# A two-layer attention trunk: x in quarters and a written order at the head, a shorter chain of norm steps at the end

## Chip, cores and metric

One core of one Trainium2 chip runs the whole kernel. The metric is device time in microseconds (us) of one execution, the median over several. Engines: TensorE (PE), VectorE (DVE), ScalarE (ACT), GpSimd (POOL), and SyncE (SP), which here only issues transfers.

## What is computed

256 tokens of width 1024 pass through two layers and a final norm, all in float32:

```python
for layer in range(2):
    h = rmsnorm(x, g_mix)
    proj = h @ w_in                      # 1024 x 7244: q,k,v of three attentions, indexer, gates
    A = stick_breaking_attention(...)    # 8 heads
    B = forgetting_attention(...)        # 8 heads, softmax with cumulative forget bias
    C = indexed_sparse_attention(...)    # rotary, indexer picks the top 64 keys per token
    y = sum(sigmoid(gate_b) * (branch_b @ w_branch[b]) for b in A, B, C)
    x = x + y @ w_out
    x = x + relu(rmsnorm(x, g_mlp) @ w_up) ** 2 @ w_down
return rmsnorm(x, g_final)               # x * (mean(x*x) + 1e-6) ** -0.5 * g_final
```

## The kernel before, in words

**Tiling.** The 256 tokens are two blocks j of 128; x lives on the chip as two halves h of its columns (`xh`, 512 columns each, both token blocks). A matrix product splits each float32 operand into a rounded part and a remainder (`whi`, `wlo` for weights, `xTh`, `xTl` for transposed activations) and sums three products (`mm3`, L117): high by high, high by low, low by high. ACT makes the high part by a copy (L91 for weights, L173 for x), DVE the low part by a subtraction (L92, L174). Weights come in `raw` tiles of four 128-row blocks (`w_rows`, L99; four buffers) and are split two row blocks at a time into four `whi` and four `wlo` buffers.

**The head.** SP issues x's first half as two transfers (L64), the norm gain (L66), the first weight tile row block by row block (`loads=4`, L104), x's second half (L62), then the next weight tiles. `norm_in` (L157) transposes x on PE, four 128x128 blocks to a PSUM tile (L168), ACT and DVE make `xTh` and `xTl` with the gain folded in, and ACT sums squares (L178). `rstd_of` (L182) makes the reciprocal root on GpSimd in three steps. The first products are the 1100 columns of C's projections in three groups: 364 and 368 columns together (`stream_groups`, L242; four row blocks k of the first group, four of the second, then the other four of each), then 368 alone (L244). `ct_done` (L237) copies each finished group out of PSUM on ACT, scaled by the norm. Behind them stand the small constants of the rotary embedding (L246 to L307).

**What sets the order.** Each engine issues its instructions in one fixed sequence. That sequence is made by a planner when the program is built: it simulates the program and picks, for an engine that comes free, by the order of the source and by what is ready. A region marked `manual_schedule(engines=...)` makes the named engines issue that region's instructions as they are written; where instructions from outside the region fall among them stays the planner's. Before, only one such region exists per layer, for PE alone (L651).

**The tail.** In layer 1's last product (`w_down`, L711) the second column half finishes token block 0 first, then block 1 (`split_last`). For each block DVE adds the residual (L713), ACT sums squares (L716), DVE multiplies by the final gain (L717), GpSimd adds the two halves' sums, makes the mean and takes the power (L185, L186, L188), ACT scales one column half (L723) and DVE the other (L725), and SP issues both outputs (L724, L726).

## Time and profile before

| | |
|---|---|
| median of 3 runs | 888.93 us (888.49 to 889.79) |
| profiled execution | 889.98 us, span 888.3 us |
| PE busy | 873.0 us, 98% of the span |
| DVE, ACT, POOL busy | 621.6, 531.1, 113.9 us |
| DMA | 150.97 MB, mean 170 GB/s |

The span runs from the first to the last instruction of the profiled execution. A busy PE is not PE at its peak, since the ends of pipelined matmuls are modelled; the start of one matmul to the start of the next shows the rate.

### The profile page before, as it was taken

How to read it: one execution, taken by the hardware profiler on the slowest of the kernel's cores; microseconds unless marked ns; L12 is line 12 of the kernel's file. 1: busy time of each engine (PE TensorE's matmuls, PEld its weight loads, DVE VectorE, ACT ScalarE, POOL GpSimd, SP SyncE). 2: the span in 40 equal slices, each digit the busy share in tenths (PEclk: the TensorE clock that was granted, in tenths of full speed). 3: DMA queues.
4: the chain of work that ended last, by engine and by line, in shares of the span. 5: the costliest groups of instructions: out<-in, count | busy, mean ns of one | idle time of the engine just before them, and what ended most of it. 6: DMA issues, size and time to landing. Idle time of an engine off the chain costs nothing.

```text
span 888.3 us, 13911 instructions
## 1 busy us (share of the span) xinstructions
PE 873.0 (98%) x5342; PEld 789.1 (89%) x5342; DVE 621.6 (70%) x1008; ACT 531.1 (60%) x874; POOL 113.9 (13%) x216
## 2 busy tenths in 40 slices
PE   7999999999999999999999999999999999999996
PEld 7998998888889999888899989988888999998885
DVE  5899787978766666545468987789876676664552
ACT  6766886776455555444365758677755655553442
POOL 2300321234001000000011014022600100000001
PEclk9999999999999999999999999999999999999998
DMA  8744544354555555555466463453346555555521
GB/s 288 244 147 143 190 143 143 116 169 143 190 190 164 176 183 190 190 189 190 137 208 195 139 197 136 143 189 128 106 150 232 169 190 190 190 188 192 190 95 48
DMA packets 102482, 150.97 MB, mean 170 GB/s; under 512 B 2928, under 2 KB 58256, under 8 KB 102416
## 3 DMA queue, kind: packets, MB, share of 16 engines
q1 hardware_dynamic: 102416, 150.08, 51.5%
q8 instruction: 42, 0.69, 0.3%
q14 instruction: 24, 0.20, 0.1%
HBM read 149.02 MB, written 1.05 MB: 169 GB/s over the span
## 4 chain that ended last, share of the span: by engine, by line
PE 92%; DVE 4%; ACT 1%; DMA 1%; issue 1%; SPq 0%; POOL 0%; POOLq 0%; ACTq 0%
PE mm L120 26%; PE mm L119 26%; PE mm L121 26%; PE av L454 2%; PE pT L438 2%; PE at L120 1%; PE at L121 1%; PE at L119 1%; DVE wlo L92 1%; DVE qs L145 1%; PE xtp L168 1%; ACT qs L143 1%; DMA x<-in_x_dram 1%; PE za L347 0%; PE yTp L579 0%
## 5 line engine op out<-in xcount | busy, mean ns | idle before, releaser
L92 DVE TENSOR_TENSOR wlo<-raw,whi 128x1024 fp32r<-128x1024 f32 (+3 forms) x289 | 347.8, 1206 | 201.0 <-ACT whi L91 199.4
L91 ACT ACTIVATE whi<-raw 128x1024 fp32r<-128x1024 f32 (+3 forms) x289 | 298.5, 1036 | 253.1 <-PE mm L121 142.4
L121 PE MATMUL mm<-xTh,wlo 128*128 128x256 f32 x752 | 214.0, 285 | 0.0
L119 PE MATMUL mm<-xTh,whi 128*128 128x256 f32 x752 | 213.8, 284 | 0.0
L120 PE MATMUL mm<-xTl,whi 128*128 128x256 f32 x752 | 213.6, 284 | 0.0
L119 PEld LDWEIGHTS mm<-xTh,whi 128*128 128x128 f32 x752 | 144.2, 192 | 0.2
L120 PEld LDWEIGHTS mm<-xTl,whi 128*128 128x128 f32 x752 | 144.2, 192 | 0.2
L121 PEld LDWEIGHTS mm<-xTh,wlo 128*128 128x128 f32 x752 | 144.2, 192 | 0.0
L120 PE MATMUL mm<-wlo,xTh 128*128 128x512 f32 (+2 forms) x320 | 122.7, 384 | 0.5 <-DVE wlo L92 0.5
L121 PE MATMUL mm<-whi,xTl 128*128 128x512 f32 (+2 forms) x320 | 121.6, 383 | 0.0
L119 PE MATMUL mm<-whi,xTh 128*128 128x512 f32 (+2 forms) x320 | 119.4, 383 | 0.3 <-ACT xTh L173 0.3
L121 PE MATMUL mm<-whi,ul 128*128 128x512 f32 x256 | 99.7, 389 | 0.0
L120 PE MATMUL mm<-wlo,uh 128*128 128x512 f32 x256 | 99.6, 389 | 0.0
L119 PE MATMUL mm<-whi,uh 128*128 128x512 f32 x256 | 99.2, 389 | 0.0
L120 PEld LDWEIGHTS mm<-wlo,xTh 128*128 128x128 f32 x320 | 61.0, 191 | 10.3 <-DVE wlo L92 1.3
L119 PEld LDWEIGHTS mm<-whi,xTh 128*128 128x128 f32 x320 | 60.9, 190 | 10.2 <-ACT xTh L173 0.7
L121 PEld LDWEIGHTS mm<-whi,xTl 128*128 128x128 f32 x320 | 60.8, 190 | 9.0
L185 POOL TENSOR_TENSOR ms<-ss 128x2 f32<-128x2 f32 (+1 forms) x6 | 4.3, 718 | 474.4 <-ACT junk L178 297.7
L121 PEld LDWEIGHTS mm<-whi,ul 128*128 128x128 f32 x256 | 48.1, 188 | 10.0
L120 PEld LDWEIGHTS mm<-wlo,uh 128*128 128x128 f32 x256 | 48.1, 188 | 10.0
L119 PEld LDWEIGHTS mm<-whi,uh 128*128 128x128 f32 x256 | 48.1, 188 | 9.7
L487 POOL TENSOR_SCALAR e<-e,rs 128x128 f32<-128x128 f32 x64 | 43.2, 693 | 27.2 <-DVE rs L484 27.2
(215 smaller groups left out, 1274.0 us busy)
## 6 DMA issues: line engine op xcount, KB each, us to landing
raw<-in_w_in_dram SPq DMA_DIRECT2D x48, 1024.0 KB, 5.0
raw<-in_w_up_dram SPq DMA_DIRECT2D x32, 1024.0 KB, 5.1
raw<-in_w_down_dram SPq DMA_DIRECT2D x32, 1024.0 KB, 5.0
raw<-in_w_branch_dram SPq DMA_DIRECT2D x12, 1024.0 KB, 5.0
raw<-in_w_out_dram SPq DMA_DIRECT2D x8, 1024.0 KB, 5.0
raw<-in_w_in_dram SPq DMA_DIRECT2D x8, 736.0 KB, 5.4
raw<-in_w_in_dram SPq DMA_DIRECT2D x3, 728.0 KB, 4.3
out_dram<-x SPq DMA_DIRECT2D x4, 256.0 KB, 2.2
```

The lines of the kernel that those rows point to most:

```text
L91: act.activation(h3[:, i:i + m], raw[:, i:i + m], AF.Copy)
L92: dve.tensor_sub(l3[:, i:i + m], raw[:, i:i + m], h3[:, i:i + m].bitcast(F32))
L119: pe.matmul(o, ah, bh, start=start, stop=False)
L120: pe.matmul(o, ah, bl, start=False, stop=False)
L121: pe.matmul(o, al, bh, start=False, stop=stop)
L143: act.activation(dst[half(i), :, i, :], src[half(i)], AF.Copy, scale=scale)
L145: dve.scalar_tensor_tensor(dst[half(1 - i), :, i, :], src[half(i)], scale, dst[half(i), :, i, :].bitcast(F32), op0=OP.mult, op1=OP.subtract)
L168: pe.transpose(p[:, i * 256 + j * 128:i * 256 + j * 128 + 128], xs[j][h][:, c:c + 128], ident)
L185: pool.tensor_add(ms, ss[:, :, 0], ss[:, :, 1])
L438: pe.transpose(p[:, q * 128:q * 128 + 128], e[:, i, q * 128:q * 128 + 128], ident)
L454: pe.matmul(o[:, c + c0:c + 256], v, p[:, a:b], start=s == 0 and n == 0, stop=s == 1 and n == 1)
L487: pool.tensor_scalar(e[:, i, c:c + n], e[:, i, c:c + n], rs[:, i, j:j + 1], 1.0, op0=OP.mult, op1=OP.mult)
```

## The change

Head:
- x comes in four quarters of 256 columns, both token blocks in one transfer (`load_x(queue, q)`).
- The gain, x's second quarter and two of the eight first weight row blocks are issued by ACT, the rest by SP; the four row blocks of both first groups are separate transfers (`head_rows`), except the last two of the second group, which share one. Each row block is split alone, when the stream comes to it (`ws[i]()`).
- A `manual_schedule` region for PE, ACT and DVE reaches from the first transposes through both column groups and the rotary constants. In it, `head_mid` says where the remaining transposes, the squares, the norm and its row form stand between the matmuls. The third group of 368 columns is now written behind the region.
- All transposes of the head use the `pt` PSUM buffers, where one half used `at`.

Tail:
- Block sums of the second column half are made in two quarters of 256 columns; the squares go to four columns of sums `fs`, one of which already has `D * EPS` added; one DVE operation adds three numbers, GpSimd takes one power (the factor 32 = sqrt(1024) is folded into the gain once).
- The scalings of both blocks are written behind both blocks' sums; ACT issues the half that it scaled, SP the one that DVE scaled.

```diff
@@ -56,14 +56,15 @@
 
     xh = [const.tile([128, 2, 512], F32, name=f"x{h}") for h in range(2)]
     xs = [[xh[h][:, j, :] for h in range(2)] for j in range(2)]
-    gload = const.tile([16, 128], F32, name="gload", tag="gload")
-
-    def load_x(h):
-        dma.dma_start(xh[h], AP(x, h * 512, [[D, 128], [128 * D, 2], [1, 512]]))
-
-    for j in range(2):
-        dma.dma_start(xh[0][:, j, :], AP(x, j * 128 * D, [[D, 128], [1, 512]]))
-    dma.dma_start(gload, AP(g_mix, 0, [[128, 16], [1, 128]]))
+    gload = const.tile([48, 128], F32, name="gload", tag="gload")
+
+    def load_x(queue, q):
+
+        queue.dma_start(xh[q // 2][:, :, (q % 2) * 256:(q % 2) * 256 + 256],
+                        AP(x, q * 256, [[D, 128], [128 * D, 2], [1, 256]]))
+
+    act.dma_start(gload[0:16], AP(g_mix, 0, [[128, 16], [1, 128]]))
+    load_x(dma, 0)
 
 
     ident = const.tile([128, 128], F32, name="ident")
@@ -71,42 +72,55 @@
     pool.affine_select(ident, ident, [[-1, 128]], OP.not_equal, 1.0, base=0, channel_multiplier=1)
     gT = const.tile([128, 32], F32, name="gT")
 
-    def g_cols(src, c):
+    def g_cols(r, c):
         p = at_tile("gps")
-        pe.transpose(p[:, 0:16], src, ident[0:16, 0:16])
+        pe.transpose(p[:, 0:16], gload[r:r + 16], ident[r:r + 16, r:r + 16])
         dve.tensor_copy(gT[:, c:c + 16], p[:, 0:16])
 
-    g_cols(gload, 0)
     mhalf = const.tile([128, 2], F32, name="mhalf")
     pool.memset(mhalf, -0.5)
 
 
...
+
+    def head_rows(off, n):
+
+        raw = raw_tile(4, n)
+        two = {}
+
+        def load(queue, i, m=1):
+            queue.dma_start(raw[:, i:i + m, :], AP(w_in, off + i * 128 * COLS, [[COLS, 128], [128 * COLS, m], [1, n]]))
+
+        def part(i):
+            if i % 2 == 0:
+                two[i // 2] = [wp.tile([128, 1024], F32R, name=t, tag=t, bufs=4) for t in ("whi", "wlo")]
+            h, l = [t[:, i % 2 * n:i % 2 * n + n] for t in two[i // 2]]
+            act.activation(h, raw[:, i], AF.Copy)
+            dve.tensor_sub(l, raw[:, i], h.bitcast(F32))
+            return h, l
+
+        return load, [lambda i=i: part(i) for i in range(4)]
 
     def w_cols(src, off, rs):
 
@@ -159,8 +173,8 @@
         xt = pair_tiles(8, "xT", 8)
         ss = small.tile([128, 2, 2], F32, name="ss")
 
-        def part(h):
-            for kp in range(2):
+        def part(h, kps=(0, 1), squares=True):
+            for kp in kps:
                 p = banks[h]("xtp")
                 for i in range(2):
                     for j in range(2):
@@ -173,7 +187,7 @@
                     act.activation(hi, p[:, i * 256:i * 256 + 256], AF.Copy, scale=g)
                     dve.scalar_tensor_tensor(lo, p[:, i * 256:i * 256 + 256], g, hi.bitcast(F32),
                                              op0=OP.mult, op1=OP.subtract)
-            for j in range(2):
+            for j in range(2 * squares):
                 junk = small.tile([128, 512], mybir.dt.bfloat16, name="junk", tag="junk", bufs=1)
                 act.activation(junk, xs[j][h], AF.Square, accum_out=ss[:, j, h:h + 1])
 
@@ -197,7 +211,7 @@
         o = [[t(), t()] for t in (mm_tile, at_tile)[:len(groups)]]
         for k0 in range(0, nk, 4):
             for g, (off, n) in enumerate(groups):
-                ws = first if first and not (k0 or g) else w_rows(src, off, rs, k0, n)
+                ws = list(first[g]) if first and not k0 else w_rows(src, off, rs, k0, n)
                 order = [(i, j) for i in range(4) for j in range(2)]
                 end = k0 + 4 == nk
                 if split_last and end:
@@ -206,6 +220,8 @@
                     if mid is not None:
                         mid(k0, g, q)
                     k = k0 + i
+                    if callable(ws[i]):
+                        ws[i] = ws[i]()
                     mm3(o[g][j][:, :n], blk(lhs, k, j * 128, j * 128 + 128), ws[i], k == 0, k == nk - 1)
                 if done is not None and end:
                     done(g, o[g])
@@ -214,38 +230,73 @@
     att = None
     for layer in range(DEPTH):
         wi0 = layer * D * COLS
+        cgs = [(736, 364), (0, 368)]
+        rstd = rb = rhalf = None
         if layer == 0:
-            wfirst = w_rows(w_in, C0 + 736, COLS, 0, 364, loads=4)
-            load_x(1)
-            xt, ss, part = norm_in(0, (at_tile, pt_tile))
-            part(0)
-            part(1)
-        rstd = rstd_of(ss)
+            head = [head_rows(C0 + c, n) for c, n in cgs]
+            (load0, _), (load1, _) = head
+            load0(act, 0)
+            load0(dma, 1)
+            load_x(act, 1)
+            load0(dma, 2)
+            load0(act, 3)
+            load1(dma, 0)
+            load1(dma, 1)
+            load1(dma, 2, 2)
+            load_x(dma, 2)
+            load_x(dma, 3)
+            xt, ss, part = norm_in(0, (pt_tile, pt_tile))
+            order = tc.manual_schedule(engines={mybir.EngineType.PE, mybir.EngineType.Activation, mybir.EngineType.DVE})
+            order.__enter__()
+            g_cols(0, 0)
+            part(0, (0,), False)
+
         with tc.tile_pool(name=f"att{layer}", bufs=1, reuse_waits="tile") as att:
             work = att
 
-            rp = at_tile("rp")
-            for j in range(2):
-                pe.transpose(rp[:, j * 128:j * 128 + 128], rstd[:, j:j + 1].to_broadcast([128, 128]), ident)
-            rb = small.tile([128, 272], F32, name="rb", tag="rb", bufs=1)[:, 0:256]
-            act.activation(rb, rp[:, 0:256], AF.Copy)
-
-            rhalf = small.tile([128, 2], F32, name="rhalf", tag="rhalf", bufs=1)
-            pool.tensor_scalar(rhalf, rstd, 0.5, 1.0, op0=OP.mult, op1=OP.mult)
+            def norms():
+
+                nonlocal rstd, rhalf
+                rstd = rstd_of(ss)
+                rhalf = small.tile([128, 2], F32, name="rhalf", tag="rhalf", bufs=1)
+                pool.tensor_scalar(rhalf, rstd, 0.5, 1.0, op0=OP.mult, op1=OP.mult)
+
+            def norm_row():
+
+                nonlocal rb
+                rp = pt_tile("rp")
+                for j in range(2):
+                    pe.transpose(rp[:, j * 128:j * 128 + 128], rstd[:, j:j + 1].to_broadcast([128, 128]), ident)
+                rb = small.tile([128, 272], F32, name="rb", tag="rb", bufs=1)[:, 0:256]
+                act.activation(rb, rp[:, 0:256], AF.Copy)
+
+            def head_mid(k0, g, q):
+                if (k0, g, q) == (0, 0, 2):
+                    part(0, (1,), False)
+                if (k0, g, q) == (0, 1, 4):
+                    part(1, (0, 1), False)
+                if (k0, g, q) == (0, 1, 2):
+                    part(0, ())
+                if (k0, g, q) == (0, 1, 7):
+                    part(1, ())
+                    norms()
+                if (k0, g, q) == (4, 1, 4):
+                    norm_row()
+
+            if layer:
+                norms()
+                norm_row()
 
             ct = att.tile([128, 2, 1152], F32, name="ct", tag="G", bufs=1)[:, :, 0:CN]
             def ct_done(c0, n, o):
                 for j in range(2):
                     act.activation(ct[:, j, c0:c0 + n], o[j][:, :n], AF.Copy, scale=rstd[:, j:j + 1])
 
-            cgs = [(736, 364), (0, 368)]
             stream_groups(xt, 8, w_in, [(wi0 + C0 + c, n) for c, n in cgs], COLS,
-                          done=lambda g, o: ct_done(*cgs[g], o), first=wfirst if layer == 0 else None)
-            ct_done(368, 368, stream_tok(xt, 8, w_in, wi0 + C0 + 368, COLS, 368))
-
+                          done=lambda g, o: ct_done(*cgs[g], o), first=None if layer else [h for _, h in head],
+                          mid=None if layer else head_mid)
             if layer == 0:
-                gload2 = const.tile([16, 128], F32, name="gload2", tag="gload")
-                dma.dma_start(gload2, AP(g_mlp, 0, [[128, 16], [1, 128]]))
+                dma.dma_start(gload[32:48], AP(g_mlp, 0, [[128, 16], [1, 128]]))
                 pos = const.tile([128, 2], I32, name="pos")
                 dma.dma_start(pos, AP(positions, 0, [[1, 128], [128, 2]]))
                 bfg = const.tile([128, DEPTH, NH], F32, name="bfg")
@@ -304,7 +355,10 @@
                 dve.tensor_scalar(rot[:, :, 0, :], trig[:, :, 0, :], -1.0, None, op0=OP.mult)
                 dve.tensor_copy(rot[:, :, 1, :], trig[:, :, 0, :])
 
-                g_cols(gload2, 16)
+                g_cols(32, 16)
+                order.__exit__(None, None, None)
+
+            ct_done(368, 368, stream_tok(xt, 8, w_in, wi0 + C0 + 368, COLS, 368))
 
 
             for c, nh in ((QI, 5), (QC, 10)):
@@ -704,26 +758,39 @@
             if last:
                 gfb = mlp.tile([128, D], F32, name="gfb")
                 dma.dma_start(gfb, AP(g_final, 0, [[0, 128], [1, D]]))
-                ss = small.tile([128, 2, 2], F32, name="ss")
+
+                act.activation(gfb, gfb, AF.Copy, scale=32.0)
+                fs = mlp.tile([128, 2, 4], F32, name="fs")
+                ms = mlp.tile([128, 2], F32, name="fms")
+                rl = mlp.tile([128, 2], F32, name="frstd")
             else:
                 xt, ss, part = norm_in(layer * 8 + 8, (at_tile, pt_tile))
             for cg in range(2):
                 o = stream_tok(uT, 32, w_down, layer * DFF * D + cg * 512, D, 512, split_last=last and cg == 1)
-                for j in range(2):
-                    dve.scalar_tensor_tensor(xs[j][cg], o[j], r2[:, j:j + 1], xs[j][cg], op0=OP.mult, op1=OP.add)
-                    if last:
+                if not last:
+                    for j in range(2):
+                        dve.scalar_tensor_tensor(xs[j][cg], o[j], r2[:, j:j + 1], xs[j][cg], op0=OP.mult, op1=OP.add)
+                    part(cg)
+                    continue
+                for j in range(2):
+                    steps = 2 if cg else 1
+                    n = 512 // steps
+                    for h in range(steps):
+                        xv = xs[j][cg][:, h * n:h * n + n]
+                        dve.scalar_tensor_tensor(xv, o[j][:, h * n:h * n + n], r2[:, j:j + 1], xv, op0=OP.mult, op1=OP.add)
                         junk = small.tile([128, 512], mybir.dt.bfloat16, name="junk", tag="junk", bufs=1)
-                        act.activation(junk, xs[j][cg], AF.Square, accum_out=ss[:, j, cg:cg + 1])
-                        dve.tensor_mul(xs[j][cg], xs[j][cg], gfb[:, cg * 512:cg * 512 + 512])
-                if not last:
-                    part(cg)
-                for j in range(2):
-                    if last and cg == 1:
-                        rl = rstd_of(ss[:, j:j + 1, :])
-                        act.activation(xs[j][1], xs[j][1], AF.Copy, scale=rl)
-                        dma.dma_start(AP(out, j * 128 * D + 512, [[D, 128], [1, 512]]), xs[j][1])
-                        dve.tensor_scalar(xs[j][0], xs[j][0], rl, None, op0=OP.mult)
-                        dma.dma_start(AP(out, j * 128 * D, [[D, 128], [1, 512]]), xs[j][0])
+                        act.activation(junk[:, :n], xv, AF.Square, accum_out=fs[:, j, cg + h:cg + h + 1])
+                    dve.tensor_mul(xs[j][cg], xs[j][cg], gfb[:, cg * 512:cg * 512 + 512])
+                    if cg == 0:
+                        dve.tensor_scalar(fs[:, j, 0:1], fs[:, j, 0:1], D * EPS, None, op0=OP.add)
+                        continue
+                    dve.tensor_scalar(ms[:, j:j + 1], fs[:, j, 1:2], fs[:, j, 0:1], fs[:, j, 2:3], op0=OP.add, op1=OP.add)
+                    pool.tensor_tensor(rl[:, j:j + 1], ms[:, j:j + 1], mhalf[:, 0:1], op=OP.pow)
+                for j in range(2 * cg):
+                    act.activation(xs[j][0], xs[j][0], AF.Copy, scale=rl[:, j:j + 1])
+                    act.dma_start(AP(out, j * 128 * D, [[D, 128], [1, 512]]), xs[j][0])
+                    dve.tensor_scalar(xs[j][1], xs[j][1], rl[:, j:j + 1], None, op0=OP.mult)
+                    dma.dma_start(AP(out, j * 128 * D + 512, [[D, 128], [1, 512]]), xs[j][1])
 
 
 _INS = ["x", "positions", "g_mix", "w_in", "b_forget", "w_branch", "w_out", "g_mlp", "w_up", "w_down", "g_final"]
```

## Rows read from the trace of the kernel before

**Rows 1.** The page, parts 1 and 4: totals, and the last chain by engine.
```profile
...
PE 873.0 (98%) x5342; PEld 789.1 (89%) x5342; DVE 621.6 (70%) x1008; ACT 531.1 (60%) x874; POOL 113.9 (13%) x216
...
PE 92%; DVE 4%; ACT 1%; DMA 1%; issue 1%; SPq 0%; POOL 0%; POOLq 0%; ACTq 0%
...
```

**Rows 2.** Windows of the head: engines (busy us, x instructions), granted clock, DMA share, GB/s.
```profile
...
0.00:5.00 5.00, 0.22 (x2) 0.22 (x2) 0.35 (x2) 2.59 (x5) 3.55 (x27) 1.00 0.55 162
...
10.00:15.00 5.00, 4.92 (x19) 4.93 (x20) 3.18 (x6) 4.85 (x11) 1.29 (x4) 1.00 1.05 373
...
```

**Rows 3.** Timeline of the head, TensorE: start us, us, engine, line, operation, idle before.
```profile
...
4.96 1.97 PE L168 MATMUL xtp<-ident,x 128*128 128x128 f32 x8
...
7.21 0.67 PE L119 MATMUL mm<-whi,xTh 128*128 128x364 f32 x1 [0.28 <-ACT xTh L173]
...
10.08 1.97 PE L168 MATMUL xtp<-ident,x 128*128 128x128 f32 x8 [0.68 <-DMA x<-in_x_dram]
...
```

**Rows 4.** The chain of waits in the head: start us, us, what.
```profile
...
12.04 0.30 PE mm L119
...
14.78 0.30 PE mm L119
...
15.27 0.17 PE mm L121
...
```

**Rows 5.** Timeline around the boundary between the first groups, ACT and TensorE.
```profile
...
22.72 0.82 ACT L91 ACTIVATE whi<-raw 128x736 fp32r<-128x736 f32 x1 [0.79 <-PE mm L121]
24.28 1.02 ACT L239 ACTIVATE ct<-mm,rstd 128x364 f32<-128x364 f32 x2 [0.73 <-PE mm L121]
...
28.52 0.33 PE L119 MATMUL mm<-whi,xTh 128*128 128x368 f32 x1
...
```

**Rows 6.** Instruction groups of the head by shape: busy us, mean ns, idle before.
```profile
...
L92 DVE TENSOR_TENSOR wlo<-raw,whi 128x736 fp32r<-128x736 f32 x8 | 7.3, 926 | 3.3 <-ACT whi L91 3.3
...
L174 DVE SCALAR_TENSOR_TENSOR xTl<-xtp,gT,xTh 128x256 fp32r<-128x256 f32 x8 | 3.6, 475 | 1.6 <-ACT xTh L173 1.6
...
L92 DVE TENSOR_TENSOR wlo<-raw,whi 128x364 fp32r<-128x364 f32 x2 | 1.0, 536 | 1.1 <-ACT whi L91 1.1
...
L91 ACT ACTIVATE whi<-raw 128x364 fp32r<-128x364 f32 x2 | 1.0, 507 | 0.6 <-DMA raw<-in_w_in_dram 0.6
...
```

**Rows 7.** Timeline of layer 1's head, TensorE and ACT.
```profile
...
450.23 0.82 PE L168 MATMUL xtp<-ident,x 128*128 128x128 f32 x6
...
450.75 0.47 ACT L173 ACTIVATE xTh<-xtp,gT 128x256 fp32r<-128x256 f32 x1 [0.35 <-PE xtp L168]
...
```

**Rows 8.** DMA issues of the head: KB each, us to landing.
```profile
...
x<-in_x_dram SPq DMA_DIRECT2D x2, 256.0 KB, 2.9
...
```

**Rows 9.** Timeline of the tail, all engines.
```profile
...
879.51 0.39 PE L121 MATMUL mm<-whi,ul 128*128 128x512 f32 x1
...
880.46 0.49 DVE L725 TENSOR_SCALAR x<-x,rstd 128x512 f32<-128x512 f32 x1 [1.01 <-POOL rstd L188]
880.86 0.75 DVE L713 SCALAR_TENSOR_TENSOR x<-mm,r,x 128x512 f32<-128x512 f32 x1
...
881.70 0.63 ACT L716 ACTIVATE junk<-x 128x512 bf16<-128x512 f32 x1 [0.52 <-DVE x L713]
...
882.46 0.69 DVE L717 TENSOR_TENSOR x<-x,gfb 128x512 f32<-128x512 f32 x1 [0.85 <-ACT junk L716]
...
883.56 0.56 POOL L188 TENSOR_TENSOR rstd<-ms,mhalf 128x1 f32<-128x1 f32 x1
884.15 0.72 ACT L723 ACTIVATE x<-x,rstd 128x512 f32<-128x512 f32 x1 [1.73 <-POOL rstd L188]
...
885.04 0.43 SPq L724 DMA_DIRECT2D out_dram<-x  x1
```

**Rows 10.** Window of the tail, and the landing of the last output line.
```profile
...
882.00:884.00 2.00, 0.00 (x0) 0.00 (x0) 0.69 (x1) 0.42 (x2) 1.33 (x3) 0.50 0.62 235
...
DMA to landing us min/median/max: 2.3/2.3/2.3
```

More of the change, by code (lines that the diff above doesn't have):

```diff
@@ L72, in trunk_kernel, with split @@
     gT = const.tile([128, 32], F32, name="gT")
-    def g_cols(src, c):
+    def g_cols(r, c):
         p = at_tile("gps")
-        pe.transpose(p[:, 0:16], src, ident[0:16, 0:16])
+        pe.transpose(p[:, 0:16], gload[r:r + 16], ident[r:r + 16, r:r + 16])
         dve.tensor_copy(gT[:, c:c + 16], p[:, 0:16])
-    g_cols(gload, 0)
     mhalf = const.tile([128, 2], F32, name="mhalf")
     pool.memset(mhalf, -0.5)
-    def split(raw, k, n, steps=1):
+    def split(raw, k, n):
         hi = wp.tile([128, 1024], F32R, name="whi", tag="whi", bufs=4)
@@ L88, in split @@
         l3 = lo[:, :k * n].rearrange("p (k n) -> p k n", k=k)
-        m = k // steps
-        for i in range(0, k, m):
-            act.activation(h3[:, i:i + m], raw[:, i:i + m], AF.Copy)
-            dve.tensor_sub(l3[:, i:i + m], raw[:, i:i + m], h3[:, i:i + m].bitcast(F32))
+        act.activation(h3, raw, AF.Copy)
+        dve.tensor_sub(l3, raw, h3.bitcast(F32))
         return h3, l3
@@ L97, in raw_tile, with w_rows @@
         return raw[:, :k * n].rearrange("p (k n) -> p k n", k=k)
-    def w_rows(src, off, rs, k0, n, loads=1):
+    def w_rows(src, off, rs, k0, n):
         raw = raw_tile(4, n)
-        m = 4 // loads
-        for i in range(0, 4, m):
-            dma.dma_start(raw[:, i:i + m, :], AP(src, off + (k0 + i) * 128 * rs, [[rs, 128], [128 * rs, m], [1, n]]))
+        dma.dma_start(raw, AP(src, off + k0 * 128 * rs, [[rs, 128], [128 * rs, 4], [1, n]]))
         r = []
         for q in range(2):
-            h, l = split(raw[:, 2 * q:2 * q + 2, :], 2, n, 2 if loads == 4 and q == 0 else 1)
+            h, l = split(raw[:, 2 * q:2 * q + 2, :], 2, n)
             r += [(h[:, i, :], l[:, i, :]) for i in range(2)]
         return r
+    def head_rows(off, n):
[11 more added lines that the diff above has]
+        return load, [lambda i=i: part(i) for i in range(4)]
     def w_cols(src, off, rs):
```

## The prediction

> **What bounds the kernel now.** I read the page's totals first: TensorE is busy 98% of the 888.3 us span and carries 92% of the chain that ended last [rows 1]. So the change can move the time only where TensorE stands still or runs slowly. Such places are at the two ends, which are what the diff edits, so I then read head and tail in the windows and the timeline.
>
> Head. The first weight matmul starts at 7.21, after eight transposes from 4.96; from 9.4 TensorE waits for the second half of x, transposes it from 10.08, and from there runs without a gap [rows 3]. The DMA engines are 0.55 busy in the window 0 to 5 and full (1.05) in 10 to 15 [rows 2]. Both windows grant a clock of 1.00, yet matmuls of 364 columns follow each other at 0.30 us up to 14.78 and at 0.17 from 15.27 [rows 4]: 1.2 GHz first, 2.4 GHz later. My marker for the head is the start of the third column group, at 28.52 [rows 5]; behind it TensorE is full, so what the head loses there the end loses.
>
> Tail. The last matmul starts at 879.51 (its result is out at about 879.9). Token block 1's residual sum starts only at 880.86, because VectorE first took block 0's scaling at 880.46. Then follow the square, GpSimd's sum, mean and power, the scaling at 884.15, the last issue at 885.04 and its landing 2.3 us later [rows 9, 10].
>
> **The change, head.** The same 96 matmuls, 16 transposes, copies and bytes remain. What changes is the order: PE, ACT and DVE now issue the whole two-group stretch as written, and a blocked instruction blocks what is written behind it on its engine. I follow it in steps.
>
> (1) x's first quarter is 256 KB and first in SP's queue, as the first half block is now: landing 2.9 us after issue [rows 8], about 3.7. The gain's transfer is issued on ACT at once and needed only afterwards. Four transposes at 1.97/8 = 0.246 us [rows 3] end at 4.7; the copy waits for all four (layer 1's copy waits, until 450.75, for the fourth, whose columns ended 0.3 before [rows 7]). Two copies (0.47 and, back to back, about 0.37) and the weight copy (0.43 back to back, 0.51 alone [rows 6]) put the first matmul at 6.2: 1.0 earlier.
>
> (2) Its six matmuls (the second waits half a microsecond for VectorE's 0.54 [rows 6]) end at 8.4. Only then are the next four transposes written; they end at 9.4, and on ACT two xT copies stand ahead of the next weight copy: 0.3 of latency, 0.84, 0.43. TensorE stands still 1.6 us, until 11.0, though x and weights have landed. Before, it resumed at 11.70 with the other eight transposes already done: the lead is gone.
>
> (3) Thirty matmuls, with another half microsecond's wait, end at 16.6 if all go at 0.167. If the slow spacing lasts to 14.2 (before, it lasted to 15.1, three microseconds behind the first matmul after the gap [rows 4]), they end at 17.9. I take 17.2.
>
> (4) x's second half: eight transposes (spacing 0.11, the row at 450.23 [rows 7]) and then, written ahead of the next weight copy, four xT copies: 0.44 + 0.3 + 1.57 + 0.43 until 20.0. TensorE idles 1.9 and another 0.5 for VectorE; twelve matmuls end at 22.5.
>
> (5) Behind these ACT has one weight copy (0.43), two squares (0.75 each, as in the tail, 881.70 to 882.46 [rows 9]), then the first copy of the next tile (0.82 [rows 5]): the first matmul starts at 22.8, and its second operand, VectorE's 0.93 [rows 6], comes at 23.7. 24 matmuls end at 27.5.
>
> (6) At the boundary to the second group ACT must issue the two `ct` copies (1.02, waiting for the matmuls) before the second group's weight copy. Before, the planner put one weight copy ahead of them, at 22.72 against 24.28 [rows 5]. The first `ct` copy can start half a microsecond before the last matmul of the other token block ends: both done at 28.3, weights at 29.1, VectorE at 30.0; 24 matmuls, with the row transposes, end at 34.0. Against 28.52 that is 5.5 later.
>
> What can cover it: the third group stands outside the fixed order, so the planner may put its copies and matmuls into the gaps. In (6) ACT is idle four microseconds, two weight buffers are free and a third PSUM buffer exists: one token block, 12 matmuls or 2.0 us, fits, and perhaps 0.4 of the wait behind it. 5.5 - 2.4 = +3.1, which I take, as nearest to the rows of the planner filling ([rows 5]). The ends: nothing filled, +5.5; everything in (4) to (6) filled, +0.5; and if TensorE hardly waits, down to -3 (of what half speed costs now, 16 matmuls x 0.137 + 17 transposes x 0.135 = 4.5 us, two thirds).
>
> Four transfers move to ACT's queue. An issue is 0.43 us [rows 9]; four cost ACT 1.7 us beside its table load, both done by about 3.9, while its first copy comes at 4.9: hidden. If the load stood ahead of them, the first weights would land 1.3 later, and (1) would lose 0.5 at most. By the window 0 to 5, with one queue, half the engines' time is free, so a second queue might land x and the weights sooner: a start at 5.8, and +2.7 for +3.1.
> The Trainium skill ("DMA: Bandwidth & Descriptors", Issuing engines are not separate DMA queues) speaks against that: transfers issued from several engines run on the same 16 engines, and only issue time is saved. By it the start stays at 6.2 and the head at +3.1; no trace here has two queues.
>
> The rotary constants (some 20 small VectorE operations and a table load) move into the fixed order, ahead of the third group: hidden, since that group takes TensorE 8 us; at worst 2 us, if they land in front of a weight copy that is due.
>
> **The change, tail.** Halving block 1's sum: VectorE 0.48 + 0.42 for 0.75 (by the 128x256 row from PSUM [rows 6]), but the squares overlap: 1.4 us against 1.5 to the last square. GpSimd's sum and mean, which fill 882.46 to 883.56 = 1.1, become one tiny VectorE operation of about 0.2 with its hand-over. It is written behind the gain multiply of 0.69 [rows 9]: it saves 0.9 if it goes ahead of that and 0.2 if not. Block 0's scaling is written later, but it was written behind block 1's sum before, too, and the planner hoisted it; of the stall of 0.96 (879.9 to 880.86) all goes, or only 0.2 if it is hoisted again. ACT's own issue saves about 0.13. The sum runs from 0.6 to 2.1. All four outputs may now be issued within 1.7 us; the engines were 0.62 busy for two microseconds with half of the bytes [rows 10], so the second half can queue behind the first: no gain over about 1.6. I take 1.2.
> The final gain's scaling by 32 (one ACT copy of 128x1024) lies in the last stage, where ACT waits between weight copies: nothing, or 1 us if it blocks one.
>
> **Sum.** +3.1 - 1.2 = +1.9. On the profiled execution's 889.98 that is 891.9; that execution lies 1.05 above the median of 888.93, so on the median: 890.8.
>
> **Rivals.**
> (a) Nothing fills the gaps, or the clock falls back in one: +5.5 - 1.2 = +4.3, 893.2. For: ACT's order as written, and a granted clock of 0.50 in the window 882 to 884, behind the last matmul [rows 10]. Against: the planner is free with the third group.
> (b) The planner covers (4) to (6): +0.5 - 1.2, 888.2, no change. For: before, it kept TensorE full from 10.08 on. Against: the third group's weights land behind two other tiles, too late for (4).
> (c) The other side: the head gains. TensorE starts at 5.6 to 6.2 and the copies keep up, so that it reaches 2.4 GHz near 10 instead of 15, and the marker comes 2 us earlier: 888.93 - 2 - 1.4 = 885.5. It decides at under 2 us of idle time between the first weight matmul and the marker. Against it: ACT's order as counted.
> (d) Transposes do not lift the clock: eight ran from 10.08, and the slow spacing still lasted three microseconds of matmuls [rows 3, 4]. Then (3) ends at 17.9: +3.8 - 1.2, 891.5. Against: layer 1's transposes at 0.11, which is faster than 0.246 by more than half [rows 7].
> The Trainium skill ("TensorE: Matmul & The Clock Gate", Part 4: PE-mode transpose) has (d) as a rule: a transpose does not count as busy work in the same way. The rows leave it open.
>
> **How the numbers follow.** Forecast (889.3 to 892) 0.30; (a) 0.20; (b) 0.20; (c) 0.24; (d) 0.06. 0.2% is 1.8 us, about what can be told from no change. Slower: (a), (d) and two thirds of the forecast, 0.46. Same: (b) and the rest of the forecast, 0.30. Faster: (c), 0.24. The range reaches through most of (c) and (a): 885.8 to 893.4; the forecast's own is 889.3 to 892.
>
> **What would show it.** In the changed trace: first weight matmul near 6.2; TensorE idle from about 9.4 to 11 behind ACT's two xT copies; an idle stretch behind the second half's transposes; third-group matmuls, or nothing, between the two groups of the second four weight rows; the two groups' last matmul past 30. In the tail: block 1's sum directly after the last matmul, and one power per block without GpSimd's sums. The prediction is wrong if TensorE has under 2 us of idle time between its first weight matmul and the marker, or if the tail from the last matmul on is not 0.6 to 2.1 us shorter.

## Result and profile after

The changed kernel takes 902.72 us (median of four runs, 901.24 to 902.86) against 889.13 for the kernel before beside it: ratio 1.0149, interval 1.0131 to 1.0167. It is slower, as forecast, but by 13.6 us instead of 1.9, and outside the range. The profiled execution has a span of 900.9.

The page of the changed kernel, parts 1 and 4, beside [rows 1]: TensorE has as many instructions as before and is busy 5.3 us longer, and the span is 12.6 longer.

```profile
...
PE 878.3 (97%) x5342; PEld 792.4 (88%) x5342; DVE 622.7 (69%) x1017; ACT 532.2 (59%) x882; POOL 112.5 (12%) x212
...
PE 88%; DVE 5%; issue 1%; ACT 1%; POOL 0%; POOLq 0%; ACTq 0%
...
```

So there is both standing still and slower running. The timeline of TensorE in the head, beside [rows 3 to 5], shows each; in brackets is the idle time before and who ended it.

```profile
...
7.10 0.67 PE L133 MATMUL mm<-whi,xTh 128*128 128x364 f32 x1 [2.29 <-ACT whi L119]
...
9.36 1.06 PE L182 MATMUL xtp<-ident,x 128*128 128x128 f32 x4
12.40 0.67 PE L133 MATMUL mm<-whi,xTh 128*128 128x364 f32 x1 [1.98 <-ACT whi L119]
...
17.38 0.51 PE L133 MATMUL mm<-whi,xTh 128*128 128x364 f32 x1
17.68 0.40 PE L134 MATMUL mm<-wlo,xTh 128*128 128x364 f32 x1
...
19.78 0.33 PE L134 MATMUL at<-wlo,xTh 128*128 128x368 f32 x1
19.95 0.33 PE L135 MATMUL at<-whi,xTl 128*128 128x368 f32 x1
20.12 1.03 PE L182 MATMUL xtp<-ident,x 128*128 128x128 f32 x8
24.12 0.44 PE L133 MATMUL at<-whi,xTh 128*128 128x368 f32 x1 [2.97 <-ACT whi L119]
...
27.32 0.51 PE L133 MATMUL at<-whi,xTh 128*128 128x368 f32 x1
27.62 0.51 PE L134 MATMUL at<-wlo,xTh 128*128 128x368 f32 x1
...
28.18 0.33 PE L133 MATMUL mm<-whi,xTh 128*128 128x364 f32 x1
28.34 0.33 PE L134 MATMUL mm<-wlo,xTh 128*128 128x364 f32 x1
...
33.71 0.43 PE L133 MATMUL at<-whi,xTh 128*128 128x368 f32 x1 [1.38 <-ACT whi L89]
34.67 0.50 PE L134 MATMUL at<-wlo,xTh 128*128 128x368 f32 x1 [0.53 <-DVE wlo L90]
...
37.42 0.51 PE L134 MATMUL at<-wlo,xTh 128*128 128x368 f32 x1
37.72 0.51 PE L135 MATMUL at<-whi,xTl 128*128 128x368 f32 x1
...
38.57 0.51 PE L133 MATMUL mm<-whi,xTh 128*128 128x368 f32 x2
...
```

Between its first weight matmul and the third group TensorE stands still four times, 1.98 + 2.97 + 1.38 + 0.53 = 6.9 us, where before it was 0.68. And the matmuls start 0.30 apart, instead of 0.17, in three stretches: up to 17.7, from 24.1 to 27.9 and from 34.7 to 38.0. Among the 96 matmuls of the first two groups, 45 follow another by over 0.2 us without an idle stretch between (17 before); over 0.168 each that sums to 7.3 us (2.5 before). So the head lost 6.2 us to standing and 4.8 to late starts. About 1.0 of the 4.8 is waiting, too: behind three of the restarts the second matmul comes 0.57 us after the first, because VectorE's remainder is late, and the third 0.47 after that. The other 3.8 are slow running: about 44 matmuls at 0.30, where before there were 16. The windows of the same stretch (columns as in [rows 2]) show the clock falling behind the last two long waits:

```profile
...
15.00:20.00 5.00, 5.00 (x24) 5.00 (x23) 0.54 (x1) 0.31 (x1) 0.00 (x0) 1.00 0.48 148
20.00:25.00 5.00, 1.89 (x12) 1.38 (x11) 2.65 (x6) 3.11 (x8) 0.00 (x0) 0.97 0.00 0
25.00:30.00 5.00, 5.00 (x22) 5.00 (x22) 1.84 (x3) 2.20 (x5) 1.35 (x4) 0.69 0.61 169
30.00:35.00 5.00, 3.09 (x18) 2.55 (x17) 1.31 (x2) 3.07 (x6) 0.21 (x1) 0.99 0.58 195
35.00:40.00 5.00, 5.00 (x23) 4.92 (x22) 4.45 (x16) 1.86 (x4) 0.00 (x0) 0.67 0.70 219
...
```

A grant of 0.69 over five microseconds is 1.2 GHz for about three and 2.4 GHz for the rest, which is what the starts show.

What TensorE waited for stands on ACT, in its timeline:

```profile
...
3.86 1.28 ACT L187 ACT_TABLE_LOAD   x1 [3.86 <-DVE gT L78]
5.16 0.47 ACT L187 ACTIVATE xTh<-xtp,gT 128x256 fp32r<-128x256 f32 x1
6.18 0.47 ACT L187 ACTIVATE xTh<-xtp,gT 128x256 fp32r<-128x256 f32 x1 [0.55 <-DVE xTl L188]
6.55 0.50 ACT L119 ACTIVATE whi<-raw 128x364 fp32r<-128x364 f32 x1
...
20.76 0.47 ACT L187 ACTIVATE xTh<-xtp,gT 128x256 fp32r<-128x256 f32 x1 [5.45 <-PE xtp L182]
21.78 0.84 ACT L187 ACTIVATE xTh<-xtp,gT 128x256 fp32r<-128x256 f32 x2 [0.55 <-DVE xTl L188]
23.20 0.47 ACT L187 ACTIVATE xTh<-xtp,gT 128x256 fp32r<-128x256 f32 x1 [0.58 <-DVE xTl L188]
23.57 0.90 ACT L119 ACTIVATE whi<-raw 128x368 fp32r<-128x368 f32 x2
...
31.93 1.02 ACT L293 ACTIVATE ct<-mm,rstd 128x364 f32<-128x364 f32 x2 [4.70 <-PE mm L135]
32.84 2.93 ACT L89 ACTIVATE whi<-raw 128x736 fp32r<-128x736 f32 x4
...
48.53 1.07 ACT L293 ACTIVATE ct<-mm,rstd 128x368 f32<-128x368 f32 x2 [0.19 <-PE mm L135]
...
```

Three things are to be seen. ACT's next weight copy stands behind the xT copies and the `ct` copies, as written; ACT itself is idle 5.45 and 4.70 us ahead of them. The second copy out of one PSUM tile comes 1.02 behind the first: DVE's copy of the same tile stands between them. And the third group's `ct` copies start at 48.53, where the kernel before has them at 36.24, so 12.3 of the loss is here:

```profile
...
36.24 1.07 ACT L239 ACTIVATE ct<-mm,rstd 128x368 f32<-128x368 f32 x2 [0.44 <-PE mm L121]
...
```

The tail, beside [rows 9]:

```profile
...
892.48 0.39 PE L135 MATMUL mm<-whi,ul 128*128 128x512 f32 x1
...
892.90 0.88 DVE L780 SCALAR_TENSOR_TENSOR x<-mm,r,x 128x256 f32<-128x256 f32 x2 [0.24 <-PE mm L135]
893.39 0.72 ACT L790 ACTIVATE x<-x,frstd 128x512 f32<-128x512 f32 x1 [1.64 <-POOL frstd L788]
...
894.02 0.40 ACT L782 ACTIVATE junk<-x 128x256 bf16<-128x256 f32 x1
...
895.15 0.69 DVE L783 TENSOR_TENSOR x<-x,gfb 128x512 f32<-128x512 f32 x1 [0.97 <-ACT junk L782]
895.76 0.27 DVE L787 TENSOR_SCALAR fms<-fs 128x1 f32<-128x1 f32 x1
896.11 0.55 POOL L788 TENSOR_TENSOR frstd<-fms,mhalf 128x1 f32<-128x1 f32 x1 [2.75 <-DVE fms L787]
896.69 0.72 ACT L790 ACTIVATE x<-x,frstd 128x512 f32<-128x512 f32 x1 [1.57 <-POOL frstd L788]
...
```

From the last matmul to the last scaling it is 4.21 us (4.64 before), to the end of the span 8.42 (8.79). The sum now starts at once, but ACT takes block 0's scaling ahead of block 1's squares, and DVE the multiply ahead of the sum of three.

### The profile page after: what moved, and what is told of

It is laid out like the page before. It is cut to its first block, busy times and chain, and to the rows that moved or that the text cites. A ratio compares the mean times of both kernels' runs of the same rounds, so it can differ in the third digit from the quotient of the medians.

```text
span 900.9 us, 13928 instructions
## 1 busy us (share of the span) xinstructions
PE 878.3 (97%) x5342; PEld 792.4 (88%) x5342; DVE 622.7 (69%) x1017; ACT 532.2 (59%) x882; POOL 112.5 (12%) x212
## 3 DMA queue, kind: packets, MB, share of 16 engines
q10 hardware_dynamic: 880, 1.17, 0.4%
HBM read 149.02 MB, written 1.05 MB: 167 GB/s over the span
## 4 chain that ended last, share of the span: by engine, by line
PE 88%; DVE 5%; issue 1%; ACT 1%; POOL 0%; POOLq 0%; ACTq 0%
PE mm L134 25%; PE mm L133 25%; PE mm L135 25%; PE av L508 2%; PE pT L492 2%; DVE wlo L90 1%; PE at L134 1%; PE at L135 1%; PE at L133 1%; DVE qs L159 1%; PE xtp L182 1%; ACT qs L157 0%; PE za L401 0%; PE yTp L633 0%; PE za L402 0%
## 5 line engine op out<-in xcount | busy, mean ns | idle before, releaser
L90 DVE TENSOR_TENSOR wlo<-raw,whi 128x1024 fp32r<-128x1024 f32 (+2 forms) x284 | 344.2, 1215 | 199.4 <-ACT whi L89 197.8
L89 ACT ACTIVATE whi<-raw 128x1024 fp32r<-128x1024 f32 (+2 forms) x284 | 294.5, 1042 | 245.1 <-PE mm L135 136.9
L133 PEld LDWEIGHTS mm<-whi,xTh 128*128 128x128 f32 x320 | 61.2, 192 | 14.6 <-ACT whi L119 5.1
L199 POOL TENSOR_TENSOR ms<-ss 128x2 f32<-128x2 f32 x4 | 2.9, 728 | 312.0 <-ACT junk L192 312.0
```

The lines of the kernel that those rows point to most:

```text
L89: act.activation(h3, raw, AF.Copy)
L90: dve.tensor_sub(l3, raw, h3.bitcast(F32))
L133: pe.matmul(o, ah, bh, start=start, stop=False)
L199: pool.tensor_add(ms, ss[:, :, 0], ss[:, :, 1])
```

## Experiments

My theory after the traces: the written order on ACT (and with it DVE) makes the loss, through the waits and the clock that falls behind them. Rivals: TensorE's written order, the transfers (quarters, two queues), the tail, and the PSUM tiles alone.

**Order for PE only.** `engines={PE}` in place of the three.

> The changed kernel (902.7 us) with the fixed order for TensorE alone; ScalarE and VectorE go back to the planner, everything else as in the change. Theory A: the written order of ScalarE and VectorE made TensorE wait (9.2 us idle in the head) and so lost the fast clock. Then most of the 13.5 us goes: 888 to 894 us, TensorE idle under 3 us between its first weight matmul and the third column group. Theory B: the smaller transfers on two queues bring the data late. Then it stays at 899 to 903. Theory C: TensorE's own written order is the cause. Then it also stays above 898.

889.41 us, ratio 1.0010 (1.0001 to 1.0019); idle behind the first weight matmul 0.57. Freeing ACT and DVE together takes back 13.3 us; no run frees one of them alone. TensorE's written order and the transfers cost next to nothing, by the interval at most 0.2%.

**No fixed order.** The region goes; quarters and two queues stay.

> The changed kernel without any fixed order in the head; quarters of x, two queues and the later third group stay. Theory A: 887 to 891 us. Theory B (transfers): 899 to 903, as the change. Theory C (TensorE's order): as A here, but well below the kernel with the order kept for TensorE alone.

889.06, ratio 1.0000 (0.9990 to 1.0009): with the new tail, but no order, the new transfers change nothing that the time could show. By the Trainium skill ("DMA: Bandwidth & Descriptors", Issuing engines are not separate DMA queues) that was to be expected; the run agrees.

**The tail alone**, on the kernel before; and later **the head alone**, with the tail of before.

> The kernel before with the change's final norm alone. By the traces the tail became 0.4 us shorter from the last matmul to the end: 888.3 to 889.3, not to be told from before (889.1). Rival: the final norm, with its 1024-column scaling copy and ScalarE issuing outputs, costs something elsewhere: 890 or more. As forecast before the change: 887.9 (1.2 us less).

> The change's head with the tail of before. Theory: head and tail add up, the tail is worth 0.4 (by the two traces) to 1.1 (e3 by medians), so 903.1 to 903.8; idle times and slow stretches of the head as in the changed kernel. Rival: the tail's own order gives nothing behind this head, 902.7.

888.01, ratio 0.9993 (0.9984 to 1.0002), and 902.28, ratio 1.0146 (1.0130 to 1.0161). The head carries the whole loss. The expected 903.1 did not come, and the rival of 902.7 is nearer; but this does not show that the tail gains nothing. In e4's trace the end of the span stands 8.83 behind the last matmul, against 8.42 in the changed kernel, so the 0.4 is there. Its third `ct` copies came at 47.73 and not 48.53, because fewer matmuls of the first stretch ran slowly (the second half's transposes start at 19.29 for 20.12), and its four runs spread over 2.3 us.

**Weights first.** Still three engines in written order, but each weight copy stands ahead of the xT copies and the next tile's two ahead of the `ct` copies (the two places, condensed):

```diff
+ for m in range(i, 1 if (g, i) == (0, 0) else 4): ws[m] = ws[m]()   # ahead of mid()
+ if first and q == 2 and steps[s + 1][0]: weights(*steps[s + 1])    # next tile
```

> The changed kernel with the fixed order of all three engines kept, but written differently: each weight copy stands ahead of the transposed-x copies that follow it in time, and the next tile's two weight copies stand ahead of the ct copies. Theory A in its narrow form (it is the places of the weight copies in the order, not that there is an order): 889 to 894 us, the stalls at the group boundary and before the ninth weight block gone. Rival: a fixed order on ScalarE and VectorE costs 10 us or more however it is written: 899 or more. Theory B (transfers): 899 to 903.

889.00, ratio 1.0001 (0.9992 to 1.0010). Behind the first weight matmul TensorE has no idle stretch until 44 us. ACT's rows at the boundary now read:

```profile
...
21.23 2.22 ACT L89 ACTIVATE whi<-raw 128x736 fp32r<-128x736 f32 x3
23.36 0.99 ACT L305 ACTIVATE ct<-mm,rstd 128x364 f32<-128x364 f32 x2
...
```

So not the fixing of an order on three engines, but which order was fixed, cost 13.7 us. Two runs undo single places of it.

**Boundary only** (step 6): the second group's last two weight copies ahead of the `ct` copies. **Second half only** (step 4): the second group's first weight copies ahead of the four xT copies. Both condensed:

```diff
+ if first and (k0, g, q) == (4, 0, 2): early[4, 1] = w_rows(...)    # boundary
+ if g and callable(ws[i]): ws[i:] = [w() for w in ws[i:]]           # second half, ahead of mid()
```

> The changed kernel (902.7 us), where only the two weight copies of the second group's last four row blocks stand ahead of the ct copies in ScalarE's order. If the boundary stall of the changed trace (1.38 + 0.53 us idle, then twelve matmuls 0.138 slower each = 1.7) goes: 899.1 us. Rival: the wait only moves to another place of the same order: 901.5 to 903.

> The changed kernel with one edit: the weight copies of the second group's first four blocks stand ahead of the four second-half xT copies (step 4 of the prediction undone). Theory: the 2.97 us of idle time until 24.12 goes, but the same xT copies and squares are then late for the next weight tile, and 1.3 to 2.5 us of idle come back some 4 us later, with the boundary (1.38 + 0.53) and the slow spacing after it unchanged: 899.5 to 901.5. Rival: the order in that one place was the whole of the second stretch and nothing takes its place: 2.97 and the 12 slow intervals of 0.14 go, 898.1.

898.22 (ratio 1.0105, 1.0091 to 1.0118) and 900.56 (1.0131, 1.0117 to 1.0146): 4.5 and 2.2 of the 13.6. Not all of that is the edits'. In both traces the second half's transposes already start earlier, at 19.30 and 19.01 for 20.12, though TensorE's instructions and its waits up to there are the same: fewer matmuls of the first stretch ran slowly, and the first one came 0.15 earlier. In e7's trace 4.0 us are left for the boundary, whose idle 1.38 + 0.53 went together with the slow matmuls behind it. In the second run the stall moved on by one tile, larger than expected, and up to the boundary the edit gained nothing (the first group ends 1.07 earlier, the transposes started 1.11 earlier). Its other 1.5 us came behind the boundary, where the same wait stands but the matmuls behind it start 0.17 apart:

```profile
...
24.68 0.43 PE L133 MATMUL mm<-whi,xTh 128*128 128x364 f32 x1 [2.62 <-ACT whi L89]
...
32.64 0.43 PE L133 MATMUL at<-whi,xTh 128*128 128x368 f32 x1 [1.38 <-ACT whi L89]
33.60 0.43 PE L134 MATMUL at<-wlo,xTh 128*128 128x368 f32 x1 [0.53 <-DVE wlo L90]
...
34.04 0.33 PE L133 MATMUL at<-whi,xTh 128*128 128x368 f32 x1
34.20 0.33 PE L134 MATMUL at<-wlo,xTh 128*128 128x368 f32 x1
...
```

The grant from 30 to 35 us is 1.00 there. Why the clock stayed up behind this wait, and fell behind the same one in the changed kernel, no run shows.

**Keep the clock.** The changed kernel, with matmuls added whose results nobody reads: 5, 12 and 6 of 512 columns, written into the idle stretches.

> The changed kernel with 5, 12 and 6 matmuls of 512 columns, whose results nobody reads, written into three of TensorE's idle stretches (about 10, 21 and 32 us), sized to fit into them; nothing else changes. Theory: part of the loss is not the idle time but the slow clock behind it; the matmuls behind the last two stretches (24 at 0.138 slower) then run fast, and the seventeen slow ones behind the first may: 902.7 - 3.3 = 899.4, down to 897. Rival: the clock stays as it was and the added matmuls only cost: 903 to 905.

```profile
...
9.92 2.26 PE L277 MATMUL fill<-xTh 128*128 128x512 f32 x5
...
18.56 3.02 PE L277 MATMUL fill<-xTh 128*128 128x512 f32 x12
...
29.12 1.52 PE L277 MATMUL fill<-xTh 128*128 128x512 f32 x6
...
```

898.34, ratio 1.0107 (1.0093 to 1.0121): 4.4 us faster with 23 more matmuls. Apart from the waits, every weight matmul from about 13 us on now starts 0.17 behind the last. The gain is the clock's, since ACT's order was not edited. It is a little more than the change lost by the clock: e8 has about 9 slow matmuls left, where the kernel before has 16 and the changed kernel 44. At the second half's transposes e8 is 2.4 us ahead (17.77 for 20.12). Behind the second and the last long wait the fast matmuls give 1.5 us each, and 0.8 is lost between them, where the next copies are now late.

**A PSUM tile for each transposed row block.**

```diff
- p = banks[h]("xtp")
+ tiles = [banks[h]("xtp"), banks[h]("xtp")]   # hi and lo of block i from tiles[i]
```

> The changed kernel where the two row blocks of one transposition go to two PSUM tiles instead of one. In the changed trace ScalarE's second copy always waits 0.55 us for VectorE's read of the first one's tile. If it is the shared tile that makes the two engines take turns, each pair is 0.55 shorter; three places on TensorE's path (first matmul, second block, second half): 901.1 us, and the 0.55 waits are gone. Rival: the turns come from somewhere else (order, semaphores): 902.2 to 903, waits as before.

899.46, ratio 1.0119 (1.0103 to 1.0134). ACT's two copies now stand back to back, and the waits of 0.55 are gone:

```profile
...
4.96 0.84 ACT L188 ACTIVATE xTh<-xtp,gT 128x256 fp32r<-128x256 f32 x2
...
```

It is worth 3.3 us against 1.6 expected: idle stretches are shorter (2.29 became 1.65, 1.98 became 0.96, 2.97 became 0.87 + 0.96), and about 0.6 is the clock, up from 14.6 instead of 17.7. The effects overlap; 4.5, 2.2, 4.4 and 3.3 are not to be added.

**A written tail.** The kernel before, with the changed tail and ACT and DVE in an order in which the sum of three stands ahead of the multiply.

> The kernel before with the change's final norm (888.0 us in the last runs), its last stage written as an order for ScalarE and VectorE: the sum of three ahead of the gain multiply, block 0's VectorE scaling in the wait for block 1's squares, and block 0's ScalarE half issued by SP. By the rows the multiply (0.6 us) leaves the path, and ScalarE's issue no longer stands before the squares: last matmul to scaling 3.2 us instead of 4.2: 887.0. Rival: the outputs collide or the planner's order was as good: 888 to 889.

888.12, ratio 0.9988 (0.9979 to 0.9997); last matmul to last scaling 3.65 us instead of 4.64, where 3.2 and 887.0 us were expected. Of the gain, 0.4 went to GpSimd's power, which now ran beside DVE's multiply:

```profile
...
880.75 0.68 DVE L743 TENSOR_TENSOR x<-x,gfb 128x512 f32<-128x512 f32 x1
880.91 0.93 POOL L742 TENSOR_TENSOR frstd<-fms,mhalf 128x1 f32<-128x1 f32 x1 [2.08 <-DVE fms L741]
...
```

**Combinations.** e12: transfers of the change without an order, written tail. e15: weights first, written tail. e11: e15 with separate PSUM tiles and one tiny activation at ACT's start, so that the table load needs no gain. e14: e11 with separate tiles in x's first half alone.

> The head of e2 (quarters of x from two queues, no fixed order) with the tail of e10. e2 took 889.06 and e10 888.12 against 889.1. Theory: the two add up, 888.0 to 888.2, span 1.0 to 1.6 below e2's 887.4. Rival: the tail's gain was noise between runs, 888.7 to 889.1.

> Head as in e5 (weight copies written ahead of xT copies), with each transposed row block in a PSUM tile of its own, with one tiny activation on ACT that needs no DMA ahead of everything (so that the table load, 3.86 to 5.14 in the changed kernel, runs before gT is there), and the tail of e10. Theory: e5's head was left with one idle stretch of 2.31 us until 6.97; the early table load takes up to 1.1 of it and the separate tiles about 0.6, so the first weight matmul comes at 5.3 to 5.9 and TensorE's lead of 1.0 to 1.7 lasts to the end; with 0.9 from the tail 886.4 to 887.1 us. Rival: as in e5 a lead of about a microsecond at the third ct copies is lost again between 40 and 60 us, where TensorE waits for other engines; then only the tail is left, 888.1. Second rival: gT or x itself is late, the first weight matmul stays near 6.6.

> Head as in e5, tail as in e10: the same comparison without the earlier start. Both theories 887.9 to 888.3; if it equals e14, the 1.3 us that e14 gains in the head are worth nothing at the end.

> As e11, but with separate PSUM tiles for the first half of x alone; the second half's four pairs share tiles as in the change, so that no transpose waits for a buffer (1.88 us at 16.92 in e11). Premise of the prediction: what the head loses or gains at the third ct copies, the end loses or gains. By it the third ct copies come at about 34.3 (35.64 of e5 less 1.3 for the earlier start), 1.9 before those of the kernel before, and with the tail of e10 the median is 886.0 to 886.8. Rival: a lead is not passed on, because behind the third ct copies another engine sets the pace (in e5 DVE was busy 19.22 of the 20 us from 40 to 60, and a lead of 0.6 to 0.9 was gone); then only the tail is left, 887.9 to 888.3.

e12 takes 888.08 (ratio 0.9994, 0.9985 to 1.0003), e11 889.54 (1.0009, 1.0001 to 1.0018), e15 888.85 (0.9996, 0.9987 to 1.0005), e14 887.84 (0.9985, 0.9976 to 0.9993). e12 came as expected, e15 above its range, e14 in its rival's place. In e11 the theory and both rivals fell: the first weight matmul came at 5.70, but a wait stood in a new place, for a tile that its readers had not left, and nine slow matmuls followed it. (The profiled execution took 1.2 us more than e11's median.)

```profile
...
16.92 1.09 PE L183 MATMUL xtp<-ident,x 128*128 128x128 f32 x4 [1.88 <-DVE xTl L189]
...
```

e14 beats both kernels, though by less than 0.2% against the one before, and not clearly more than e10 does, which has a new tail alone (0.9988). So no run shows a gain from the head. Its first weight matmul starts 1.29 before e15's (6.09, 7.38), yet its third `ct` copies only 0.19 before (34.75, 34.94), and its last matmul 0.3 (878.60, 878.90). The 1.1 between them went to the clock: counted as for the changed kernel, e14 has 17 late starts that sum to 2.7 us, e15 nine that sum to 1.6. Nor is that due to the edit: e5 has e15's head and sums to 2.7, and e10 has the head of the kernel before and sums to 1.0 for its 2.5, with the third `ct` copies at 34.85 for 36.24. So a difference of a microsecond in the head between two traces can be the clock's alone.

From the third `ct` copies on, e14's lead over the kernel before goes from 1.5 to 0.9. From 40 to 60 us TensorE is busy 19.40 us in e14, 19.42 in e5 and e15, and 20.00 in the kernel before. The difference is a wait of 0.60 for DVE's `qs` at 43.17, which e5 has, too (0.58), and the changed kernel (0.48 at 56.61), but not the kernel before or e1. So this is not a lead that is lost: all ten kernels with the order on three engines lose 0.6 to 0.9 us between that marker and the last matmul, the changed kernel too (12.3 and 13.0), while e1, with TensorE's order alone, and e10 keep what they had to within 0.2 (0.2 and 0.4 ahead, 1.4 and 1.3).

## Why the prediction was wrong

The direction came out (its own chances gave "slower" 0.46), and TensorE waits where the forecast said, for the copies that it named. The term that failed is the head's in step (6), "5.5 - 2.4 = +3.1": it measured +12.3 at the marker. The 5.5 failed because the sums let the clock come up once and stay up, and priced the copies too low; the 2.4, the planner's cover, came to some 0.3.

| step: marker | predicted | measured |
|---|---|---|
| (1) first weight matmul | 6.2 | 7.10 |
| (2) matmuls resume | 11.0 | 12.40 |
| (3) thirty matmuls end | 17.2 | 20.12 |
| (4) resume behind second half | 20.0 | 24.12 |
| (4) twelve matmuls end | 22.5 | 28.18 |
| (5) 24 more end | 27.5 | 32.2 |
| (6) second group ends | 34.0 | 40.8 |

- (1): the load of ACT's table was taken to lie beside the transfers' issues. It started only with the gain and ran from 3.86 to 5.14. The second copy waited 0.55 for DVE besides.
- (2) and (4): copies were priced at the spacing of back-to-back copies. Out of one PSUM tile ACT and DVE take turns. Four copies took 2.9 us (20.76 to 23.67) and not 1.57, and the second half cost 2.97 of idle time instead of 1.9.
- (3), (4), (6): the sums let TensorE run at 2.4 GHz from 14.2 on at the latest, once and for all. The clock came up at 17.7, fell again behind 2.97 and behind 1.38 + 0.53 us of idle time, and 12 and 10 matmuls ran slowly before it came back. The thirty matmuls took 7.7 us for 6.2, the twelve 4.1 for 2.5, the last 24 of the second group 6.1 for 4.0 (with two transposes and 0.3 of the third group among them). The wait at the boundary itself was right: 2.5 us from the last matmul to the second operand. Rival (a) named a falling clock and gave it no price of its own; in e8 keeping it up gave 4.4 us.
- (5) erred the other way: 1.0 us of waiting was in the sum, and nothing waited (4.0 us for 5.0). The slow matmuls ahead had given the copies time; in e8, where these ran fast, the stretch took 4.8.
- The cover: 2.4 us were expected of the planner, by [rows 5], where it had put weight copies ahead of `ct`. It put two third-group matmuls there, at 38.57, some 0.3 us, and none into ACT's idle 4.70. The third group's first weights were there: their transfer was issued at 13.84 and such a one takes 4.2. "Two weight buffers are free" did not hold for it, as far as e7 shows: there the planner did put the third group's first copy ahead of `ct`, at 29.56, but the copy waited (1.17) for a matmul half way through the first group. That place is 30.2 in the changed kernel, which leaves 1.7 of ACT's 4.70. Why not even these were filled no run shows; that belongs to the planner.
- The marker: the loss of 12.3 was passed on in full, and 0.7 came on top (last matmul 12.97 later). The premise holds for gains as well (e10: 1.4 and 1.3); the 0.7 is a second cost of the order on three engines, which stood in no term; 0.48 of it is the wait for `qs`. DVE is busier there: 19.2 of the 20 us from 40 to 60 in e5, 18.25 in the kernel before.
- The tail took off 0.4, below its bounds of 0.6 to 2.1, so this sign failed too: the stall of 0.96 went as hoped, but "0.2 if not" came true for the sum of three, and ACT's hoisted scaling (0.72 ahead of the squares) was in no term.
- The base: 1.05 us were taken off for a profiled execution above its median; that of the changed kernel was not above its own, which makes one of the missing microseconds. e10's trace, with the same head, is 1.4 ahead of it at the marker: that execution had its clock up late.

Sum: steps (1) to (6) 6.8 (40.8 for 34.0) and the cover 2.4 are the 9.2 between +3.1 and +12.3 at the marker; with 0.7 between marker and last matmul, 0.8 of the tail and the base's 1.05 it is 11.7 of the 11.9 us by which the forecast was low.

## What to carry to other kernels

Where an order is written out for a copying engine, write the copy that the next matmul needs ahead of copies that wait for a matmul: the same region cost 13.6 us or nothing by that alone. Price a wait of TensorE twice, for the time it stands and for the matmuls behind it at half clock, and look whether ACT and DVE read one PSUM tile in turn. A planner that filled gaps before need not fill those around a fixed order. And before a microsecond in the head is put down to an edit, compare the traces ahead of the edited place: here one and the same head differed by 1.1 to 1.5 us through the clock alone.

## What was not expected of the hardware

- ACT's first table load can wait for its activation's operand: in the changed kernel it started at 3.86, with the gain, and took 1.28. With a first activation that waits for nothing, as in e11, it ran from 2.77. It need not wait: in the kernel before it ran at 0.78, though its activation had x only at 3.42, and in e2 at 2.79, with the activation at 5.33. What decides no run shows.
- When the clock comes up differs between executions of one head: late starts sum to 2.5 us in the kernel before and 1.0 in e10, to 2.7 in e5 and 1.6 in e15. Behind the same 1.38 + 0.53 us of waiting it fell in the changed kernel and stayed up in e13.
- The granted clock reads 1.00 in the windows up to 20 us, though matmuls start 0.30 apart until 17.7; after that the column and the starts of the changed kernel agree.
- One GpSimd power of 128x1 took 0.55 us alone and 0.87 to 0.93 beside DVE's 128x512 multiply.
- ACT's and DVE's copies of one PSUM tile never overlap here (5.16 to 5.63, 5.67 to 6.15, 6.18 on); from two tiles they do. The Trainium skill ("PSUM — Partial Sum Buffer", PSUM bank collisions raise a hardware error) says that two engines must not access one bank at once and that software keeps them apart; the rows agree, and whether program or chip made the wait no run here shows.
